# Decoder step on one core: sums of weight blocks added in the SBUF chunk in place of sums kept in DRAM, with five plain column tiles in place of seven

## The chip, the cores and the metric

The kernel runs on one core of one Trainium2 chip. The metric is the device time of one launch in microseconds, the median of three runs. The engines are named as in the profile: PE (TensorE; PEld is its weight load), DVE (VectorE), ACT (ScalarE), POOL (GpSimd) and SP (SyncE, which here only starts transfers).

## What is computed

One decoder layer for 576 tokens (64 sample tokens and 512 prompt tokens) at a model width of 1024. Only the last part, a feed-forward block of width 2816, is touched by the change:

```python
D_FF = int(math.ceil(8 * D_MODEL / 3 / 256) * 256)      # 2816
...
xn = rms_norm(x, g[4])
gate, up = jnp.split(xn @ w_ffn_in, 2, axis=-1)
x = x + rms_norm((jax.nn.silu(gate) * up) @ w_ffn_out, g[5])
```

Ahead of it stand the input projections with a gated convolution and a linear recurrence, a merge, and a cross-attention into 256 memory tokens.

## The kernel before

**Products.** All matrices are float32. A weight chunk of up to 1024 columns by 128 partitions is loaded into a buffer `wraw` (five buffers), split by ACT into a rounded part `whi` and by DVE into the rest `wlo` (four buffers each), and a product takes three matmuls (hi by hi, hi by lo, lo by hi; `mm3`, lines 105 to 108). The activations lie transposed, 128 channels by 576 tokens, in units named `u`, also as a high and a low part.

**Halves.** Tokens are cut in two ways. In the plain way half 0 holds 320 tokens and half 1 holds 256. In the other way both halves, L and R, hold 288.

**The feed-forward block** has 22 column tiles of 128 columns of the gate and the same of the up matrix. The first `NB` = 7 tiles go the plain way (`ffn_half`): for each half, 8 row blocks of gate and of up, so 48 matmuls for half 1 (tokens `F0` to `F6` in `ORDER`, while half 0 is still being normalised) and 48 for half 0 (the loop over `NB` behind it). Each of these 28 steps loads its own chunk of 512 KB.

The other 15 tiles (`ffn_pair`) use seven products of half the depth in place of eight. Row blocks are called E (even) and O (odd), columns G (gate) and U (up). Each product is a block of 4 row blocks by 128 columns times 288 tokens, 12 matmuls. Its weight block is one of EG, OG, OU or a sum: s1 = EU+OU, s2 = EG+EU+OU, s3 = EG+EU, s4 = EG+OG+EU+OU. The order in a tile is EG, s1, s2, OG, s3, s4, OU. Two blocks of 256 KB share a chunk, so two tiles make seven chunks. The tokens' own sums for this are made by `x3_sums` (lines 1342 to 1353) out of x3n, the normalised input.

**Sums of weights.** Before, s1 to s4 are DRAM tensors of 512 by 1920. `sum_task` (line 547) fills them by 32 transfers of 960 KB from POOL's queue, 16 plain copies and 16 with `accum_op=add`, spread over the steps of the first 400 us by `sum_step`. A block of a sum is later loaded by SP like any other weight.

**Order.** Until the first pair step a scheduler places the instructions; steps are written out one after another, and after each step `drain` lets so much background work (norm chains, `x3_sums`) into the program as the step's `budget` allows. From the first pair step on, PE, ACT and DVE follow the written order, while the queues of SP and POOL are still placed by the scheduler. In a pair step (`run_steps`) the engines get, in this order, the 12 matmuls, one small reading of the PSUM bank (`p1` to `p7`), and half of the split of the chunk three ahead (`w_part`); `w_part` also asks for the transfers of later chunks.

**The join of the halves.** The norm of half 0 ends in `rstd_wide` (lines 856 to 860), followed by a multiplication (line 907) and a split (lines 102 and 103) for each of the 8 row blocks of x3n. The first step of half 0 reads them in order.

Of the kernel before, what the change touches and what calls it, by code (L numbers as in the profile page):

```python
# [9 lines left out]
F32 = mybir.dt.float32  # L10
F32R = mybir.dt.float32r
AF = mybir.ActivationFunctionType
ALU = mybir.AluOpType
# [8 lines left out]
DFF = 2816  # L22
# [2 lines left out]

HS = (0, 320)
HW = (320, 256)
NB = 7

# [9 lines left out]


BUD = {"mix": 390, "kv": 306, "q": 480, "o": 2214, "F": 390, "s": 696}

UNIT = 640
NUNITS = 59
# [8 lines left out]
def decoder_step(  # L53
# [7 lines left out]
    nc = tc.nc  # L61
    PE, ACT, DVE, POOL = nc.tensor, nc.scalar, nc.vector, nc.gpsimd
# [38 lines left out]
    def split(hi, lo, src):  # L101
        ACT.copy(hi, src)  # L102
        DVE.tensor_sub(lo, src, f(hi))  # L103
# [74 lines left out]
    def w_dma(upto):  # L178
        while ptr["dma"] <= min(upto, len(wsrc) - 1):
            i = ptr["dma"]  # L180
            srcs, nk, ncol, _ = wsrc[i]
            t = wraw_p.tile([128, 1024], F32, tag="wraw", name="wraw")
            n = nk * ncol // len(srcs)
            for j, src in enumerate(srcs):
                nc.sync.dma_start(out=t[:, j * n:(j + 1) * n].rearrange("p (k c) -> p k c", c=ncol), in_=src)
            raw[i] = t
            ptr["dma"] += 1

# [2 lines left out]
    def w_part(i, b, dma_ahead=2):  # L191

        if i >= len(wsrc) or (b == 0 and ptr["prep"] > i) or (b == 1 and i not in parts):
            return
        assert b or ptr["prep"] == i
        w_dma(i + dma_ahead)
        _, nk, ncol, as_is = wsrc[i]
        if as_is or nk * ncol < 1024:
            if b == 0:
                w_prep(i)  # L200
            return
        if b == 0:
# [51 lines left out]
    def step(w, pe, post=None, budget=4000, prep=True):  # L254
        steps.append((w, pe, post, budget, prep))

    def run_steps():
        nextw = 0
        manual = ExitStack()
        by_hand = False  # L260
        for w, pe, post, budget, prep in steps:
            if w:
                nextw = w[-1] + 1
            if prep in ("pair", "hand"):
                if not by_hand:
                    by_hand = True
                    drain(None)
                    w_prep(nextw - 1 + 2)
                    manual.enter_context(tc.manual_schedule(engines={PE.engine, ACT.engine, DVE.engine}))
                pe(*[ready.pop(i) for i in w])  # L270
                soon, late = post or (None, None)
                if soon:
                    soon()
                if prep == "pair":
                    w_part(nextw - 1 + 3, 0 if w else 1)
                else:
                    w_prep(nextw - 1 + 3)
                if late:
                    late()
                continue  # L280
            if not prep:
                pe()
            else:
                w_prep((w[0] if w else nextw) + 3)
                pe(*[ready.pop(i) for i in w])
            if post:
                post()
            drain(budget)
        manual.close()
# [13 lines left out]
    small = cst.tile([128, 80], F32, name="small")  # L303
# [237 lines left out]
        return g  # L541

    sums = {n: tc.dram_tile([512, DFF - NB * 128], F32, name=f"sum_{n}") for n in ("s1", "s2", "s3", "s4")}

    def sum_task(op, n, src, i):
        def go():
            r = slice(i * 128, i * 128 + 128)
            if src in sums:  # L550
                a = sums[src][r, :]
            else:
                k = 2 * i + (src[0] == "O")
                c = (src[1] == "U") * DFF
                a = w_ffn_in[0][k * 128:(k + 1) * 128, c + NB * 128:c + DFF]
            kw = {"accum_op": ALU.add} if op == "add" else {}
            tc.keep_in_program_order(nc.gpsimd.dma_start(out=sums[n][r, :], in_=a, **kw))
        return go

    sum_tasks = deque(  # L560
        sum_task(op, n, src, i)
        for stage in ((("copy", "s1", "EU"), ("copy", "s3", "EG")), (("add", "s1", "OU"), ("add", "s3", "EU")),
                      (("copy", "s2", "s3"),), (("add", "s2", "OU"),), (("copy", "s4", "s2"),), (("add", "s4", "OG"),))
        for op, n, src in stage for i in range(4))

    def sum_step():
        if sum_tasks:
            step([], sum_tasks.popleft(), budget=0)


    h_h, h_l, vv = [None] * KT, [None] * KT, [None] * KT
    box = {}

# [142 lines left out]
    for c in range(KT):  # L716
        def wi(sec):
            return [w_cols(w_in[0], 0, KT, sec * D + c * 128, 128)]
        if c == 0:
            wi(3), wi(1)  # L720
            step([1], startup, lambda: (in_u(0)[1](), in_hc(0)[1](), softplus()), budget=0, prep=False)
        else:
            step(wi(3), *in_u(c), budget=0)
            step(wi(1), *in_hc(c), budget=3000)
        if c:
            sum_step()
        step(wi(2), *in_hh(c), budget=2000)
        if c:
            sum_step()
        step([], *in_gate(c), budget=2000)  # L730
        step(wi(0), *in_hb(c), budget=9000)
        if c:
            sum_step()


    vs_h, vs_l, z1 = [None] * KT, [None] * KT, [None] * KT
# [12 lines left out]
    def br_rnn(n):  # L749
        def pe(W):  # L750
            box["yr"] = mmt()
            gemm2(box["yr"], W, full(h_h, h_l))

        def post():
            t = box.pop("sgs")
            DVE.tensor_mul(both(t), both(t), box.pop("yr")[:, :, :HN])
            z1[n] = t
            POOL.tensor_copy(small[:, n:n + 1], t[:, 0:1])
            vs_h[n], vs_l[n] = new(F32R), new(F32R)
            split(vs_h[n][:, :T], vs_l[n][:, :T], vv[n][:, :T])  # L760
            free(vv[n])
            if n == 0:
                free(gd, gr_a, gr_x)
            if n == KT - 1:
                free(h_h, h_l)
        return pe, post
# [3 lines left out]
    def br_conv(n):  # L770
        def pe(W):
            box["yc"] = mmt()
            gemm2(box["yc"], W, full(vs_h, vs_l))

        def post():
            t = box.pop("sgs")
            DVE.tensor_mul(both(t), both(t), box.pop("yc")[:, :, :HN])
            DVE.tensor_add(t[:, :T], t[:, :T], z1[n][:, :T])
            POOL.tensor_copy(small[:, n:n + 1], t[:, 0:1])
            z_h[n], z_l[n] = new(F32R), new(F32R)  # L780
            split(z_h[n][:, :T], z_l[n][:, :T], t[:, :T])
            free(t, z1[n])
            if n == KT - 1:
                free(vs_h, vs_l, xn_h, xn_l)
        return pe, post
# [18 lines left out]
    for n in range(KT):  # L804
        step([w_cols(w_in[0], 0, KT, 5 * D + n * 128, 128)], *br_gate(n, "r"))
        step([w_cols(w_rnn_out[0], 0, KT, n * 128, 128)], *br_rnn(n))
        if n == 1:
            step([], state_out)
        sum_step()
    for n in range(KT):  # L810
        step([w_cols(w_in[0], 0, KT, 4 * D + n * 128, 128)], *br_gate(n, "c"))
        step([w_cols(w_conv_out[0], 0, KT, n * 128, 128)], *br_conv(n))
        sum_step()
    assert not sum_tasks


    fb = [[None] * 2 for _ in range(4)]
# [201 lines left out]
    for h in (h0, h1):  # L1019
        for n in range(KT):  # L1020
            step([w_cols(w_mix_out[0], 0, KT, n * 128, 128)], *proj_half(n, fullh(z_h, z_l), h, 1, after_mix),
                 budget=BUD["mix"])
# [337 lines left out]
    def ffn_half(j, up, h):  # L1360
# [15 lines left out]
            free(t)  # L1376
        return pe, post

    def block(name, j):
        if name in sums:  # L1380
            src = sums[name][:, (j - NB) * 128:(j - NB + 1) * 128].rearrange("(k p) c -> p k c", p=128)
        else:
            c = (name[1] == "U") * DFF + j * 128
            src = w_ffn_in[0][:, c:c + 128].rearrange("(k e p) c -> e p k c", p=128, e=2)[name[0] == "O"]
        return src

    FF = {}

# [129 lines left out]
    for a in ORDER.split():  # L1518
        token(a)
    for j in range(NB):  # L1520
        for up in range(2):
# [4 lines left out]
    F = {}  # L1526
# [216 lines left out]
```

## Time and profile before

| | us |
|---|---|
| median of 3 runs | 1157.83 (1157.72 to 1158.13) |
| the profiled execution | 1157.59, of which the span is 1155.8 |
| PE busy | 1134.3 |
| DVE busy | 675.0 |
| ACT busy | 603.2 |
| POOL busy | 146.9 |
| DMA, mean over the span | 165 GB/s |

The span is the profiled part of the execution; the 1.8 us around it are launch and end. Busy times overlap, and a busy PE is not a PE at its peak, because its matmuls are pipelined. TensorE's granted clock is full in all slices of the page.

### The profile page before, as it was taken

What the parts mean: (1) busy time and instruction counts of PE and PEld (TensorE: products, weight loads), DVE (VectorE), ACT (ScalarE), POOL (GpSimd) and SP (SyncE); (2) the same over time, 40 slices, a digit from 0 to 9 for tenths busy, and PEclk for the clock granted to TensorE, in tenths of its full rate; (3) what the DMA queues carried; (4) which work ended last, traced back from release to release, by engine and by line L of the source; (5) the groups of instructions that cost most, each with busy time, mean ns of one, the idle gap of its engine ahead of it and who ended that gap; (6) DMA issues with size and microseconds to landing.
All of it is one profiled execution on the core that took longest, in us unless ns stands there. A gap on an engine that the chain in (4) does not pass through costs nothing.

```text
span 1155.8 us, 21040 instructions
## 1 busy us (share of the span) xinstructions
PE 1134.3 (98%) x8524; PEld 1113.9 (96%) x8524; DVE 675.0 (58%) x1082; ACT 603.2 (52%) x1030; POOL 146.9 (13%) x301
## 2 busy tenths in 40 slices
PE   6999999999999999999999999999999999999996
PEld 4999999999999999999998899999999999999996
DVE  6666666652223335698767777989314663466535
ACT  5665566652122225666557778775325552255543
POOL 4433333212001000022210000000000000000000
PEclk9999999999999999999999999999999999999999
DMA  7556787567547546567675585565444553455702
GB/s 226 171 163 191 178 186 163 177 160 170 173 141 164 147 123 187 147 193 227 196 227 189 192 274 165 155 200 164 129 126 131 164 150 107 118 164 166 227 2 83
DMA packets 256859, 191.13 MB, mean 165 GB/s; under 512 B 9432, under 2 KB 241896, under 8 KB 256634
## 3 DMA queue, kind: packets, MB, share of 16 engines
q1 hardware_dynamic: 249812, 149.95, 43.6%
q0 software_dynamic: 6144, 38.50, 13.0%
q8 instruction: 67, 1.10, 0.4%
q10 hardware_dynamic: 806, 1.34, 0.3%
q14 instruction: 30, 0.25, 0.1%
HBM read 180.36 MB, written 40.85 MB: 191 GB/s over the span
## 4 chain that ended last, share of the span: by engine, by line
PE 94%; DVE 2%; ACT 1%; DMA 1%; issue 1%; POOL 0%; SPq 0%; DVEq 0%; ACTq 0%
PE mm L107 23%; PE mm L108 23%; PE mm L106 23%; PE aux L1397 4%; PE aux L1396 4%; PE aux L1395 4%; PE aux L1225 1%; PE aux L1209 1%; PE aux L106 1%; PE aux L107 1%; PE aux L108 1%; PE mm L1397 1%; PE mm L1396 1%; PE mm L1395 1%; DMA wraw<-in_w_in_dram 1%
## 5 line engine op out<-in xcount | busy, mean ns | idle before, releaser
L106 PE MATMUL mm<-u,whi 128*128 128x288 f32 (+2 forms) x2032 | 605.3, 298 | 0.6 <-ACT u L458 0.6
L107 PE MATMUL mm<-u,whi 128*128 128x288 f32 (+2 forms) x2032 | 601.7, 296 | 0.5 <-DVE u L103 0.5
L108 PE MATMUL mm<-u,wlo 128*128 128x288 f32 (+2 forms) x2032 | 601.7, 296 | 0.2 <-POOL wlo L431 0.2
L103 DVE TENSOR_TENSOR wlo<-wraw,whi 128x1024 fp32r<-128x1024 f32 (+2 forms) x294 | 304.0, 1035 | 215.5 <-ACT whi L102 209.1
L102 ACT CAST whi<-wraw 128x1024 fp32r<-128x1024 f32 (+2 forms) x294 | 261.1, 898 | 286.6 <-PE mm L107 216.6
L107 PEld LDWEIGHTS mm<-u,whi 128*128 128x128 f32 x2032 | 384.5, 189 | 2.4 <-DVE u L103 1.3
L106 PEld LDWEIGHTS mm<-u,whi 128*128 128x128 f32 x2032 | 384.3, 189 | 2.2 <-ACT u L458 1.2
L108 PEld LDWEIGHTS mm<-u,wlo 128*128 128x128 f32 x2032 | 384.0, 189 | 0.8 <-POOL wlo L431 0.6
L1397 PE MATMUL aux<-u,wlo 128*128 128x288 f32 x360 | 106.2, 295 | 0.0
L1396 PE MATMUL aux<-u,whi 128*128 128x288 f32 x360 | 106.1, 295 | 0.0
L1395 PE MATMUL aux<-u,whi 128*128 128x288 f32 x360 | 105.9, 294 | 0.0
L102 ACT CAST u<-u 128x576 fp32r<-128x576 f32 (+6 forms) x117 | 58.9, 532 | 78.6 <-DVE u L640 26.2
L103 DVE TENSOR_TENSOR u<-u,u 128x576 fp32r<-128x576 f32 (+6 forms) x117 | 65.4, 578 | 16.8 <-ACT u L102 16.6
L1397 PEld LDWEIGHTS aux<-u,wlo 128*128 128x128 f32 x360 | 67.6, 188 | 0.0
L1395 PEld LDWEIGHTS aux<-u,whi 128*128 128x128 f32 x360 | 67.6, 188 | 0.0
L1396 PEld LDWEIGHTS aux<-u,whi 128*128 128x128 f32 x360 | 67.6, 188 | 0.0
L103 DVE TENSOR_TENSOR u<-aux,u 128x512 fp32r<-128x512 f32 (+2 forms) x60 | 32.8, 584 | 3.9 <-ACT u L102 3.8
L102 ACT CAST u<-aux 128x512 fp32r<-128x512 f32 (+2 forms) x60 | 28.0, 514 | 6.6 <-DVE u L103 2.1
L106 PE MATMUL aux<-u,u 128*128 128x256 f32 (+1 forms) x96 | 27.8, 294 | 0.0
L108 PE MATMUL aux<-u,u 128*128 128x256 f32 (+1 forms) x96 | 27.7, 289 | 0.0
L107 PE MATMUL aux<-u,u 128*128 128x256 f32 (+1 forms) x96 | 27.6, 289 | 0.0
L1425 ACT ACTIVATE u<-u 128x576 f32<-128x576 f32 x15 | 10.3, 686 | 32.9 <-DVE u L1422 32.9
(284 smaller groups left out, 1193.2 us busy)
## 6 DMA issues: line engine op xcount, KB each, us to landing
wraw<-in_w_in_dram SPq DMA_DIRECT2D x48, 512.0 KB, 4.1
sum_s<-in_w_ffn_in_dram POOLq DMA_DIRECT2D x24, 960.0 KB, 8.3
wraw<-sum_s SPq DMA_DIRECT2D x60, 256.0 KB, 3.3
wraw<-in_w_ffn_in_dram SPq DMA_DIRECT2D x28, 512.0 KB, 4.8
wraw<-in_w_ffn_in_dram SPq DMA_DIRECT2D x45, 256.0 KB, 3.3
wraw<-in_w_mix_out_dram SPq DMA_DIRECT2D x16, 512.0 KB, 3.8
wraw<-in_w_kv_x_dram SPq DMA_DIRECT2D x16, 512.0 KB, 3.8
wraw<-in_w_q_x_dram SPq DMA_DIRECT2D x16, 512.0 KB, 3.9
```

Of the source, the lines that this page charges most:

```text
L102: ACT.copy(hi, src)
L103: DVE.tensor_sub(lo, src, f(hi))
L106: PE.matmul(out, lhsT=wh, rhs=xh, start=start, stop=False)
L107: PE.matmul(out, lhsT=wh, rhs=xl, start=False, stop=False)
L108: PE.matmul(out, lhsT=wl, rhs=xh, start=False, stop=stop)
L1209: PE.transpose(ps[:, d * 256 + i * 128:d * 256 + (i + 1) * 128], kr[i][:, h * 256 + d * 128:h * 256 + (d + 1) * 128], ident)
L1225: PE.matmul(ps[0:m], lhsT=t[:, k * 64:k * 64 + m], rhs=src, **kw)
L1395: PE.matmul(ps, lhsT=wh[:, k, :], rhs=xh[x][:, xs], start=first and i == 0, stop=False, skip_group_check=True)
L1396: PE.matmul(ps, lhsT=wh[:, k, :], rhs=xl[x][:, xs], start=False, stop=False, skip_group_check=True)
L1397: PE.matmul(ps, lhsT=wl[:, k, :], rhs=xh[x][:, xs], start=False, stop=last and i == 3, skip_group_check=True)
L1425: ACT.activation(FF["t"][:, 0:T], FF["t"][:, 0:T], AF.Silu)
```

## The change

`NB` becomes 5, so tiles 5 and 6 go by products too: 17 tiles by products, 5 plain. `ORDER` ends in `F4 D0`, where `D0` drains all the background work that is left, and the budget of an `F` step becomes 800. The DRAM sums, their 32 transfers, the steps that spread them and two one-column POOL copies are gone. A block that is a sum is now built in its half of the `wraw` chunk: SP loads the first part, and POOL's queue adds one, two or three more parts of 256 KB (`accum_op=add`). A pair step asks for transfers 4 chunks ahead of the chunk that it splits, not 2.

```diff
@@ decoder_step
-NB = 7
+NB = 5
...
-    "P3 pA2 oB2 pA1 O5 V6 O4 V7 pA3 XB0 pA0 O6 O7 Z0 oB3 oA0 oA1 oA2 oA3 F0 F1 F2 F3 F4 F5 F6")
+    "P3 pA2 oB2 pA1 O5 V6 O4 V7 pA3 XB0 pA0 O6 O7 Z0 oB3 oA0 oA1 oA2 oA3 F0 F1 F2 F3 F4 D0")
-BUD = {"mix": 390, "kv": 306, "q": 480, "o": 2214, "F": 390, "s": 696}
+BUD = {"mix": 390, "kv": 306, "q": 480, "o": 2214, "F": 800, "s": 696}
@@ w_dma
-                nc.sync.dma_start(out=t[:, j * n:(j + 1) * n].rearrange("p (k c) -> p k c", c=ncol), in_=src)
+                dst = t[:, j * n:(j + 1) * n].rearrange("p (k c) -> p k c", c=ncol)
+                src = src if isinstance(src, list) else [src]
+                nc.sync.dma_start(out=dst, in_=src[0])
+                for more in src[1:]:
+                    nc.gpsimd.dma_start(out=dst, in_=more, accum_op=ALU.add)
@@ run_steps
-                    w_part(nextw - 1 + 3, 0 if w else 1)
+                    w_part(nextw - 1 + 3, 0 if w else 1, 4)
@@ sums, sum_task, sum_tasks, sum_step and their calls: taken out
@@ br_rnn and br_conv
-            POOL.tensor_copy(small[:, n:n + 1], t[:, 0:1])
@@ block
+    PARTS = {"s1": ("EU", "OU"), "s2": ("EG", "EU", "OU"), "s3": ("EG", "EU"), "s4": ("EG", "OG", "EU", "OU")}
+
     def block(name, j):
-        if name in sums:
-            src = sums[name][:, (j - NB) * 128:(j - NB + 1) * 128].rearrange("(k p) c -> p k c", p=128)
-        else:
-            c = (name[1] == "U") * DFF + j * 128
-            src = w_ffn_in[0][:, c:c + 128].rearrange("(k e p) c -> e p k c", p=128, e=2)[name[0] == "O"]
-        return src
+
+        def src(part):
+            c = (part[1] == "U") * DFF + j * 128
+            return w_ffn_in[0][:, c:c + 128].rearrange("(k e p) c -> e p k c", p=128, e=2)[part[0] == "O"]
+        return [src(p) for p in PARTS.get(name, (name,))]
```

**POOL in the pair stage.** Before, POOL's queue ends with the last of four writes of x2a and the four spills of x2; none of these belongs to a weight (`DMASW` is a wait for an earlier transfer of POOL's queue, `DMAHW` for one of SP's).

```order
L1317 DMA x2a_s_100<-u8_8626 128x640 [waits DMASW7_49,DVE_49,Activation_49]
L1473 DMA x2_s_101<-u58_9745 128x512 [waits DMASW0_49,Activation_49]
L1473 DMA x2_s_101<-u5_9804 128x512 [waits DMASW1_49,Activation_49]
L1473 DMA x2_s_101<-u28_9863 128x512 [waits DMASW2_49,Activation_49]
L1473 DMA x2_s_101<-u18_9923 128x512 [waits DMASW3_49,Activation_49]
```

Now the same queue has 119 adding transfers here. These are 12 of the 14 that two tiles take, from the seventh chunk of one pair of tiles on; a line that repeats the chunk of an earlier line and waits for `DMASW` alone is an add onto the result of that earlier add.

```order
L189 DMA wraw_10359<-in_w_ffn_in_dram 128x4x128 [waits DMAHW2_49,DMASW3_49,DVE_49]
L189 DMA wraw_10359<-in_w_ffn_in_dram 128x4x128 [waits DMASW3_49]
L189 DMA wraw_10408<-in_w_ffn_in_dram 128x4x128 [waits DMAHW5_49,DMASW7_49,DVE_49]
L189 DMA wraw_10359<-in_w_ffn_in_dram 128x4x128 [waits DMASW6_49,DMASW4_49]
L189 DMA wraw_10444<-in_w_ffn_in_dram 128x4x128 [waits DMAHW6_49,DMAHW4_49,DVE_49]
L189 DMA wraw_10444<-in_w_ffn_in_dram 128x4x128 [waits DMASW7_49]
L189 DMA wraw_10481<-in_w_ffn_in_dram 128x4x128 [waits DMASW2_49,DMAHW0_49,DMASW1_49,DVE_49]
L189 DMA wraw_10481<-in_w_ffn_in_dram 128x4x128 [waits DMAHW1_49]
L189 DMA wraw_10481<-in_w_ffn_in_dram 128x4x128 [waits DMASW2_49]
L189 DMA wraw_10566<-in_w_ffn_in_dram 128x4x128 [waits DMAHW3_49,DMAHW4_49,DMASW6_49,DVE_49]
L189 DMA wraw_10481<-in_w_ffn_in_dram 128x4x128 [waits DMASW5_49,DMASW3_49]
L189 DMA wraw_10566<-in_w_ffn_in_dram 128x4x128 [waits DMAHW5_49]
```

The queue is in order, so the third line stands behind the wait of the second, though it adds to another chunk.

**DVE at the join of the halves.** Before, the last split of half 0's x3n (the last line, `u1_8592`) had one of the `x3_sums` instructions (line 1345) ahead of it, and two splits of plain chunks.

```order
L103 TENSOR_TENSOR u38_8549<-u54_8547,u48_8548 128x320
L1374 TENSOR_TENSOR u6_9095<-u6_9095,mm_9033 128x256
L907 SCALAR_TENSOR_TENSOR u58_8584<-u8_8626,gT_79,u36_8939 128x320
L103 TENSOR_TENSOR wlo_9112<-wraw_9027,whi_9111 128x1024
L103 TENSOR_TENSOR u22_9099<-u6_9095,u34_9098 128x256
L103 TENSOR_TENSOR u26_8586<-u58_8584,u10_8585 128x320
L907 SCALAR_TENSOR_TENSOR u16_8590<-u8_8626,gT_79,u36_8939 128x320
L1345 TENSOR_TENSOR u15_8481<-u15_8481 128x288
L103 TENSOR_TENSOR wlo_9155<-wraw_9065,whi_9154 128x1024
L103 TENSOR_TENSOR u1_8592<-u16_8590,u24_8591 128x320
```

Now, counted to the same split (`u1_8540`), 14 of the 16 first instructions of `x3_sums` (lines 1311 to 1314 of the changed file) and one of their splits stand ahead of it; these are the last 12 lines.

```order
L1313 SCALAR_TENSOR_TENSOR u5_8435<-u15_8429,u5_8435 128x288
L103 TENSOR_TENSOR u26_8534<-u58_8532,u10_8533 128x320
L1313 SCALAR_TENSOR_TENSOR u40_8483<-u28_8477,u40_8483 128x288
L1311 TENSOR_TENSOR u58_8532<-u58_8532 128x288
L1313 SCALAR_TENSOR_TENSOR u54_8495<-u18_8489,u54_8495 128x288
L873 SCALAR_TENSOR_TENSOR u16_8538<-u8_8574,gT_79,u21_8850 128x320
L1314 SCALAR_TENSOR_TENSOR u40_8483<-u40_8483 128x288
L1312 TENSOR_TENSOR u58_8532<-u16_8538,u58_8532 128x288
L1314 SCALAR_TENSOR_TENSOR u54_8495<-u54_8495 128x288
L1314 SCALAR_TENSOR_TENSOR u5_8435<-u5_8435 128x288
L103 TENSOR_TENSOR u42_9012<-u28_8477,u45_9011 128x576
L103 TENSOR_TENSOR u1_8540<-u16_8538,u24_8539 128x320
```

From the first instruction of `rstd_wide` on DVE (line 859 before) to that last split there are now 37 instructions, both ends counted: 2 of `rstd_wide`, 2 chunk splits of 1024, 8 multiplications, 8 splits of 320, 1 product with its split of 256 (two), 14 of `x3_sums` and 1 split of 576.

## Rows read from the trace of the kernel before

**Rows 1.** The page: busy time of each engine, and the chain that ended last.

```profile
PE 1134.3 (98%) x8524; PEld 1113.9 (96%) x8524; DVE 675.0 (58%) x1082; ACT 603.2 (52%) x1030; POOL 146.9 (13%) x301
PE 94%; DVE 2%; ACT 1%; DMA 1%; issue 1%; POOL 0%; SPq 0%; DVEq 0%; ACTq 0%
```

**Rows 2.** Busy time by stretch: half 1's plain steps, half 0's, the products.

```profile
core 0: us, PE busy (x) PEld busy (x) DVE busy (x) ACT busy (x) POOL busy (x), PEclk, DMA share, GB/s
744.00:763.00 19.00, 19.00 (x159) 18.92 (x159) 18.29 (x26) 13.96 (x21) 2.16 (x4) 1.00 0.73 224
786.00:830.00 44.00, 43.96 (x301) 43.72 (x300) 31.78 (x48) 22.42 (x34) 0.00 (x0) 1.00 0.54 156
870.00:950.00 80.00, 80.00 (x607) 80.00 (x606) 47.30 (x81) 42.52 (x81) 0.00 (x0) 1.00 0.54 155
```

**Rows 3.** Timeline of PE: first step of half 1, of half 0, its wait.

```profile
739.48 0.28 PE L106 MATMUL mm<-u,whi 128*128 128x256 f32 x1
...
781.14 0.31 PE L106 MATMUL mm<-u,whi 128*128 128x320 f32 x1
...
784.87 0.41 PE L107 MATMUL mm<-u,whi 128*128 128x320 f32 x1 [0.34 <-DVE u L103]
```

**Rows 4.** Timeline of ACT at the join: start, us, instruction.

```profile
769.50 0.46 ACT L858 ACTIVATE u<-u 128x320 f32<-128x320 f32 x1
```

**Rows 5.** Timeline of DVE at the join: start, us, instruction.

```profile
773.04 1.47 DVE L907 SCALAR_TENSOR_TENSOR u<-u,gT,u 128x320 f32<-128x320 f32 x3
774.43 1.61 DVE L103 TENSOR_TENSOR u<-u,u 128x320 fp32r<-128x320 f32 x4
775.97 1.47 DVE L907 SCALAR_TENSOR_TENSOR u<-u,gT,u 128x320 f32<-128x320 f32 x3
...
778.17 1.21 DVE L103 TENSOR_TENSOR wlo<-wraw,whi 128x1024 fp32r<-128x1024 f32 x1
779.30 0.47 DVE L103 TENSOR_TENSOR u<-u,u 128x320 fp32r<-128x320 f32 x1
779.70 0.40 DVE L1374 TENSOR_TENSOR u<-u,mm 128x256 f32<-128x256 f32 x1
780.03 0.53 DVE L907 SCALAR_TENSOR_TENSOR u<-u,gT,u 128x320 f32<-128x320 f32 x1
...
785.81 0.44 DVE L1345 TENSOR_TENSOR u<-u 128x288 f32<-128x288 f32 x1
786.17 0.44 DVE L1348 SCALAR_TENSOR_TENSOR u<-u 128x288 f32<-128x288 f32 x1
```

**Rows 6.** Transfers of 256 KB: queue, count, KB, median us to landing.

```profile
wraw<-sum_s SPq DMA_DIRECT2D x60, 256.0 KB, 3.3
...
x_s<-u POOLq DMA_DIRECT2D x8, 256.0 KB, 3.1
...
u<-in_mem_prompt_dram SPq DMA_DIRECT2D x4, 256.0 KB, 2.5
```

**Rows 7.** DMA queues, 880 to 950 us: packets, MB, share of 16 engines.

```profile
q1 hardware_dynamic: 22607, 11.26, 55.4%
```

**Rows 8.** DMA queues and issues, 70 to 100 us, three plain copies to DRAM.

```profile
q0 software_dynamic: 432, 2.95, 29.0%
...
sum_s<-in_w_ffn_in_dram POOLq DMA_DIRECT2D x3, 960.0 KB, 7.1
```

**Rows 9.** DMA queues and issues, 344 to 390 us, four adds in DRAM.

```profile
q0 software_dynamic: 496, 3.44, 38.3%
...
sum_s<-in_w_ffn_in_dram POOLq DMA_DIRECT2D x4, 960.0 KB, 8.4
```

**Rows 10.** Line 557, POOL's transfers for the sums: ns min, median, max.

```profile
L557 POOL DMA_DIRECT2D sum_s<-in_w_ffn_in_dram x24: 517/802/907, 35.0 to 384.8; - x24
```

More of the change, by code (lines that the diff above doesn't have):

```diff
@@ L541, in gate_w @@
         return g
[L545 to L551, printed above, removed]
-            else:
[L553 to L568, printed above, removed]
     h_h, h_l, vv = [None] * KT, [None] * KT, [None] * KT
@@ L724, in decoder_step @@
             step(wi(1), *in_hc(c), budget=3000)
-        if c:
-            sum_step()
         step(wi(2), *in_hh(c), budget=2000)
-        if c:
-            sum_step()
         step([], *in_gate(c), budget=2000)
         step(wi(0), *in_hb(c), budget=9000)
-        if c:
-            sum_step()
     vs_h, vs_l, z1 = [None] * KT, [None] * KT, [None] * KT
@@ L778, in post @@
             DVE.tensor_add(t[:, :T], t[:, :T], z1[n][:, :T])
-            POOL.tensor_copy(small[:, n:n + 1], t[:, 0:1])
             z_h[n], z_l[n] = new(F32R), new(F32R)
@@ L808, in decoder_step @@
             step([], state_out)
-        sum_step()
     for n in range(KT):
@@ L812, in decoder_step @@
         step([w_cols(w_conv_out[0], 0, KT, n * 128, 128)], *br_conv(n))
-        sum_step()
-    assert not sum_tasks
     fb = [[None] * 2 for _ in range(4)]
@@ L1377, in ffn_half @@
         return pe, post
+    PARTS = {"s1": ("EU", "OU"), "s2": ("EG", "EU", "OU"), "s3": ("EG", "EU"), "s4": ("EG", "OG", "EU", "OU")}
     def block(name, j):
-        if name in sums:
-            src = sums[name][:, (j - NB) * 128:(j - NB + 1) * 128].rearrange("(k p) c -> p k c", p=128)
-        else:
-            c = (name[1] == "U") * DFF + j * 128
-            src = w_ffn_in[0][:, c:c + 128].rearrange("(k e p) c -> e p k c", p=128, e=2)[name[0] == "O"]
-        return src
+        def src(part):
+            c = (part[1] == "U") * DFF + j * 128
+            return w_ffn_in[0][:, c:c + 128].rearrange("(k e p) c -> e p k c", p=128, e=2)[part[0] == "O"]
+        return [src(p) for p in PARTS.get(name, (name,))]
     FF = {}
```

## Prediction

> **What bounds the kernel now.** I read the page first. PE is busy for 98% of the span and 94% of the chain that ended last is PE [rows 1], so PE's own instructions set the time. What shortens the time is fewer matmuls; what lengthens it is anything that makes PE wait.
>
> Then the stretches, for what a matmul costs. In each PE is busy all the time at full clock, so length over count is the price [rows 2]: 19.00/159 = 0.1195 us for 256 columns, 44.00/301 = 0.1462 us for 320, 80.00/607 = 0.1318 us for 288.
>
> Then the join of the two token halves, because the change shortens what lies ahead of it. Half 1's plain steps start at 739.48 us, half 0's at 781.14, and the last row block of the first half-0 step begins at 784.87 after a wait of 0.34 us for a DVE split [rows 3]. So the norm of half 0 arrives just in time behind seven tiles of half 1. DVE works almost without a pause there: busy 18.29 of the 19.00 us of [rows 2].
>
> Last the transfers, because the change moves sums into the stage that uses them. Between 880 and 950 us SP's loads of 512-byte rows take 55.4% of the time of the 16 DMA engines [rows 7], while POOL moves nothing there.
>
> **The change, part by part.** *Fewer matmuls.* A plain tile is 48 x (0.1195 + 0.1462) = 12.75 us, a product tile 84 x 0.1318 = 11.07 us. Two tiles change sides: -3.4 us, if PE waits no more than before.
>
> *The join.* Two tiles less of half 1 free PE by 2 x 48 x 0.1195 = 11.5 us: it could start half 0 at 781.14 - 11.5 = 769.6. What it needs is not earlier by as much. ACT's last instruction of the norm ends at 769.96 [rows 4], behind the same work in both kernels, and after it the written program has 37 DVE instructions up to the last split that the first half-0 step needs. Their prices from the starts in [rows 5]: a chunk split 1.13 us (778.17 to 779.30), a multiplication 0.463 (three from 773.04 to 774.43), a split of 320 0.385 (four from 774.43 to 775.97), a product or split of 256 0.33 (779.70 to 780.03), an instruction of `x3_sums` 0.36 (785.81 to 786.17). The split of 576 I take at 0.385 x 576/320 = 0.69, the two of the norm at 0.40 like their width. Sum: 2 x 1.13 + 8 x 0.463 + 8 x 0.385 + 2 x 0.33 + 14 x 0.36 + 0.69 + 2 x 0.40 = 16.2 us. The last split ends at 769.96 + 16.2 = 786.2, 1.3 us after its place before, though PE came 11.5 us sooner. Most of what two tiles freed on DVE (four chunk splits, 4.5 us) goes to the 5.0 us of `x3_sums` that `D0` puts ahead. PE stands for about 13 us between 769.6 and 786.2.
> Against the profiled execution this place is +1.3 us. Behind it four half-0 steps are missing, 96 x 0.1462 = -14.0 us, and two product tiles are added, +22.1 us: +9.4 us in all. If DVE were faster than I count by as much as its four missing chunk splits, the place is at -3 and this term +5; if waits for ACT's casts cost as much again as two chunk splits (2.3 us), +12.
>
> *The removed work.* 32 transfers and 16 POOL copies lie in stages where POOL is at 13% and PE does not wait for it; they cost nothing now and give back nothing. Up to the join PE, ACT and DVE have the same instructions in the same order.
>
> *The sums.* 17 tiles have 119 blocks, so 119 loads and 119 adds of 256 KB. Two tiles are seven chunks, 14 loads and 14 adds, and PE needs 22.1 us for them.
> First the DMA engines. Loads: 0.554 x 70 us = 38.8 us for 11.26 MB [rows 7], 3.44 us per MB, 0.90 us of every engine for a block of 0.262 MB. No add of this shape is in the trace. Adds of long rows are: 0.383 x 46 us = 17.6 us for 3.44 MB, 5.12 us per MB [rows 9]; copies on the same route take 0.290 x 30 us = 8.7 us for 2.95 MB, 2.95 us per MB [rows 8]. The add costs 1.74 times the copy. For 512-byte rows I take the same ratio: 1.57 us. Below, an add costs no more than a load, 0.90. 14 x (0.90 + 1.57) = 34.6 us for what PE does in 22.1.
> Then POOL's queue. Six adds of the 14 wait for the one before them, and five more issues lie between these waits, so the queue needs 6 x landing + 5 x issue. An issue is 0.80 us [rows 10]. A landing lies between 2.5 us, the fastest load of 256 KB, and 8.4 us, an add of 960 KB [rows 6, 9]. It breaks even with PE at (22.1 - 4.0)/6 = 3.0 us, just under the plain 256 KB from POOL, 3.1 us [rows 6]. Taking from the 8.4 us the long add's own movement (0.983 MB x 5.12 = 5.0 us) and putting in 1.57 gives 4.9 us, so 33.4 us. That agrees with the engines' 34.6, and I take 34.6.
> What is queued behind: a late add holds ACT's split of its half chunk, ACT stands in order, so the next readings of the PSUM banks are late, and PE stops two or three blocks later. Five buffers cannot cover a lasting rate. They are full when each of the three groups of product tiles begins, which I count as half a period each: 8.5 - 1.5 = 7 periods x (34.6 - 22.1) = 87.5 us.
> The Trainium skill (DMA: Bandwidth & Descriptors, section "Anatomy of one DMA — SWDGE (gpsimd) path") gives a transfer from POOL as 2.0 us plus its bytes over 436 GB/s; by it a block would land in an estimated 2.6 us, the queue would need 19.6 us, and the sum would be 1167. The trace does not bear it out: 3.1 us for a plain block [rows 6], and 7.1 us for a copy [rows 8] for which the fit has 4.3. The same page ("Issuing engines are not separate DMA queues") says that transfers of all issuing engines run on the same 16 engines, which is how I add loads and adds.
>
> *Sum.* 1157.6 + 9.4 + 87.5 = 1254.5 us. The profiled execution is 0.2 us under the median.
>
> **The rivals.** *Adds nearly hidden.* If adds move as fast as loads, the engines need 14 x 1.80 = 25.3 us, and 7 x 3.2 = 22 us are lost: 1189. If a landing also stays under 3.0 us, nothing is lost and only the join is left: 1167. For it: a block is small, and the longest waits are few. Against it: the 1.74 of [rows 8, 9], and a plain block that already lands at the edge.
> *The waits rule.* If short rows make an add dearer than its bytes, the landing decides. At 7 us, between 4.9 and 8.4, the queue needs 46 us: 7 x 23.9 = 167, so 1334.
> *Faster.* The first condition of the first rival, and with it the join: if the last split of half 0's x3n ended before 776, PE would stand less than 3.4 us and the time would fall below that of before, to 1154 at best. It would need DVE to do in 6 us what I price at 16.2, and its rows hardly vary.
>
> **How the numbers follow.** My forecast, queues that set the pace at 31 to 44 us, 1225 to 1325: 0.58. Adds nearly hidden, 1165 to 1225: 0.27. The waits rule, above 1325: 0.09. Faster: 0.04. Within 0.2%, about the least that a measurement of this kernel can tell from no change (1155.5 to 1160.1): 0.02. Range 1178 to 1325: below it lie 0.06 and some 0.06 of the hidden case, above it 0.09. Faster 0.04, same 0.02, slower 0.94.
>
> **What would show it.** Right: the stretch of the products longer per tile than 11.07 us; ACT casts that wait for transfers from `w_ffn_in`; POOL's transfers starting one after another at the landing of the one before; a PE gap of some 13 us at the join; DMA share near 0.9 or more in the product stage. Wrong, if a 256-KB add lands within 3 us, or if PE starts half 0 at 770 without a gap.

## Result and profile after

The changed kernel takes 1341.12 us (median of 4 runs, 1336.87 to 1343.46) against 1157.98: ratio 1.1577, interval 1.1544 to 1.1609. It was predicted slower, at 1254.5 us; the loss is 183 us, not 97, and the time lies above the range of 1178 to 1325.

From the page of the changed kernel: its engines and its chain, three groups of instructions whose waits matter here, and its 256-KB transfers with the median us from issue to landing:

```profile
PE 1171.3 (87%) x8500; PEld 1144.6 (85%) x8500; DVE 677.9 (51%) x1089; ACT 604.2 (45%) x1036; POOL 274.4 (20%) x372
...
PE 64%; issue 14%; DMA 9%; POOL 7%; DVE 2%; ACT 1%; SPq 0%; POOLq 0%; DVEq 0%; ACTq 0%
...
L102 ACT CAST whi<-wraw 128x1024 fp32r<-128x1024 f32 (+2 forms) x297 | 261.5, 889 | 490.4 <-DMA wraw<-in_w_ffn_in_dram 209.5
...
L1362 PE MATMUL aux<-u,whi 128*128 128x288 f32 x408 | 132.5, 325 | 141.3 <-ACT u L1373 136.3
L189 POOL DMA_DIRECT2D wraw<-in_w_ffn_in_dram x119 | 154.6, 1636 | 317.3 <-DMA wraw<-in_w_ffn_in_dram 290.2
...
wraw<-in_w_ffn_in_dram SPq DMA_DIRECT2D x119, 256.0 KB, 4.7
wraw<-in_w_ffn_in_dram POOLq DMA_DIRECT2D x119, 256.0 KB, 5.9
```

PE is 87% busy, not 98% [rows 1]. Read the waits as one chain: PE's products wait for ACT's reading of a PSUM bank (line 1373, 136.3 us). ACT stands ahead of that reading at a split (line 102) whose chunk has not landed (209.5 us). POOL, which issues the adds (line 189), stands 290.2 us for transfers. What it stands for is in the view of line 189:

```profile
L189 POOL DMA_DIRECT2D wraw<-in_w_ffn_in_dram x119: 1265/1452/2442, 801.2 to 1258.2; - x119
...
who waited for it (us, times):
  POOL wraw L189: 240.1, 51
  ACT whi L102: 209.5, 38
...
DMA to landing us min/median/max: 4.3/5.9/11.1
```

240.1 us of waits are adds that wait for adds, 51 times: the third and fourth parts of sums, three in each of 17 tiles. They are called chained adds below. Issuing an add keeps POOL itself busy for 1.30 us (154.6/119); that is not yet the transfer. The Trainium skill says so too (Perfetto Trace Analysis, section "DMA Instruction — SWDGE (GPSIMD)"): its recorded end is the end of making descriptors, not of moving data; here the data lands 4.3 us or more after the issue.

One period of two tiles (14 adds) in the timeline of POOL, up to the start of the next. Columns: start, us, and in brackets the time that POOL stood before:

```profile
1144.36 3.90 POOL L189 DMA_DIRECT2D wraw<-in_w_ffn_in_dram  x3 [2.55 <-DMA wraw<-in_w_ffn_in_dram]
1151.08 2.59 POOL L189 DMA_DIRECT2D wraw<-in_w_ffn_in_dram  x2 [2.82 <-DMA wraw<-in_w_ffn_in_dram]
1160.17 2.62 POOL L189 DMA_DIRECT2D wraw<-in_w_ffn_in_dram  x2 [6.49 <-DMA wraw<-in_w_ffn_in_dram]
1166.92 2.59 POOL L189 DMA_DIRECT2D wraw<-in_w_ffn_in_dram  x2 [4.12 <-DMA wraw<-in_w_ffn_in_dram]
1173.74 3.91 POOL L189 DMA_DIRECT2D wraw<-in_w_ffn_in_dram  x3 [4.23 <-DMA wraw<-in_w_ffn_in_dram]
1183.99 2.60 POOL L189 DMA_DIRECT2D wraw<-in_w_ffn_in_dram  x2 [6.34 <-DMA wraw<-in_w_ffn_in_dram]
1188.61 3.91 POOL L189 DMA_DIRECT2D wraw<-in_w_ffn_in_dram  x3 [2.03 <-DMA wraw<-in_w_ffn_in_dram]
```

From 1144.36 to 1188.61 are 44.3 us: 18.2 of issues and six stops of 26.0 together. PE needs 22.1 us for the same two tiles when it does not wait. The stretches show where PE lost time:

```profile
core 0: us, PE busy (x) PEld busy (x) DVE busy (x) ACT busy (x) POOL busy (x), PEclk, DMA share, GB/s
763.00:790.00 27.00, 21.18 (x120) 19.77 (x119) 24.24 (x50) 18.98 (x31) 0.00 (x0) 0.82 0.40 118
...
900.00:1062.00 162.00, 104.47 (x690) 101.43 (x689) 53.15 (x91) 46.48 (x86) 55.90 (x43) 0.83 0.88 157
1062.00:1106.00 44.00, 44.00 (x334) 44.00 (x333) 15.31 (x18) 8.75 (x11) 14.63 (x12) 1.00 0.76 143
1106.00:1300.00 194.00, 127.87 (x830) 125.30 (x829) 67.39 (x118) 60.01 (x119) 58.18 (x45) 0.81 0.83 154
```

At the join (763 to 790) PE stands for 5.8 us. In the two stretches that are mostly products (900 to 1062, 1106 to 1300) PE is 64 and 66% busy and the granted clock is 0.83 and 0.81; between them, where `w_ffn_out` is used, PE is full at full clock. At the join PE ends half 1 two tiles sooner, and the timeline of PE there reads:

```profile
770.67 0.28 PE L108 MATMUL mm<-u,wlo 128*128 128x256 f32 x1
774.18 1.09 PE L106 MATMUL mm<-u,whi 128*128 128x320 f32 x2 [3.23 <-ACT u L102]
...
787.00 0.42 PE L107 MATMUL mm<-u,whi 128*128 128x320 f32 x1 [1.50 <-DVE u L103]
```

The last row block of the first half-0 step begins at 787.00, before at 784.87 [rows 3]: 2.1 us later.

### The profile page after: what moved, and what is told of

It is laid out like the page before. It is cut to its first block, busy times and chain, and to the rows that moved or that the text cites. A ratio compares the mean times of both kernels' runs of the same rounds, so it can differ in the third digit from the quotient of the medians.

```text
span 1341.0 us, 21179 instructions
## 1 busy us (share of the span) xinstructions
PE 1171.3 (87%) x8500; PEld 1144.6 (85%) x8500; DVE 677.9 (51%) x1089; ACT 604.2 (45%) x1036; POOL 274.4 (20%) x372
## 4 chain that ended last, share of the span: by engine, by line
PE 64%; issue 14%; DMA 9%; POOL 7%; DVE 2%; ACT 1%; SPq 0%; POOLq 0%; DVEq 0%; ACTq 0%
PE mm L107 18%; PE mm L108 18%; PE mm L106 18%; DMA wraw<-in_w_ffn_in_dram 9%; POOL wraw L189 7%; PE aux L1191 1%; PE aux L1175 1%; PE aux L106 1%; PE aux L107 1%; PE aux L108 1%; PE aux L1362 1%; PE aux L1363 1%; PE aux L1364 1%; DVE wlo L103 0%; DVE u L103 0%
## 5 line engine op out<-in xcount | busy, mean ns | idle before, releaser
L106 PE MATMUL mm<-u,whi 128*128 128x288 f32 (+2 forms) x1968 | 587.9, 299 | 4.3 <-ACT u L102 4.3
L107 PE MATMUL mm<-u,whi 128*128 128x288 f32 (+2 forms) x1968 | 584.2, 297 | 1.7 <-DVE u L103 1.7
L108 PE MATMUL mm<-u,wlo 128*128 128x288 f32 (+2 forms) x1968 | 584.0, 297 | 1.1 <-POOL wlo L435 1.1
L103 DVE TENSOR_TENSOR wlo<-wraw,whi 128x1024 fp32r<-128x1024 f32 (+2 forms) x297 | 303.9, 1024 | 402.9 <-ACT whi L102 399.9
L102 ACT CAST whi<-wraw 128x1024 fp32r<-128x1024 f32 (+2 forms) x297 | 261.5, 889 | 490.4 <-DMA wraw<-in_w_ffn_in_dram 209.5
L106 PEld LDWEIGHTS mm<-u,whi 128*128 128x128 f32 x1968 | 373.7, 190 | 5.9 <-ACT u L102 4.8
L107 PEld LDWEIGHTS mm<-u,whi 128*128 128x128 f32 x1968 | 373.7, 190 | 4.0 <-DVE u L103 2.9
L108 PEld LDWEIGHTS mm<-u,wlo 128*128 128x128 f32 x1968 | 373.2, 190 | 1.7 <-POOL wlo L435 1.5
L1362 PE MATMUL aux<-u,whi 128*128 128x288 f32 x408 | 132.5, 325 | 141.3 <-ACT u L1373 136.3
L189 POOL DMA_DIRECT2D wraw<-in_w_ffn_in_dram x119 | 154.6, 1636 | 317.3 <-DMA wraw<-in_w_ffn_in_dram 290.2
L1362 PEld LDWEIGHTS aux<-u,whi 128*128 128x128 f32 x408 | 84.7, 208 | 147.1 <-ACT u L1373 139.7
L1363 PE MATMUL aux<-u,whi 128*128 128x288 f32 x408 | 128.9, 316 | 0.0
L1364 PE MATMUL aux<-u,wlo 128*128 128x288 f32 x408 | 128.8, 316 | 0.0
L1363 PEld LDWEIGHTS aux<-u,whi 128*128 128x128 f32 x408 | 85.2, 209 | 0.0
L1364 PEld LDWEIGHTS aux<-u,wlo 128*128 128x128 f32 x408 | 85.1, 209 | 0.0
L106 PE MATMUL aux<-u,u 128*128 128x256 f32 (+1 forms) x96 | 27.7, 294 | 0.0
L107 PE MATMUL aux<-u,u 128*128 128x256 f32 (+1 forms) x96 | 27.6, 289 | 0.0
```

The costliest lines, as they stand in the source:

```text
L106: PE.matmul(out, lhsT=wh, rhs=xh, start=start, stop=False)
L107: PE.matmul(out, lhsT=wh, rhs=xl, start=False, stop=False)
L108: PE.matmul(out, lhsT=wl, rhs=xh, start=False, stop=stop)
L189: nc.gpsimd.dma_start(out=dst, in_=more, accum_op=ALU.add)
L1362: PE.matmul(ps, lhsT=wh[:, k, :], rhs=xh[x][:, xs], start=first and i == 0, stop=False, skip_group_check=True)
L1363: PE.matmul(ps, lhsT=wh[:, k, :], rhs=xl[x][:, xs], start=False, stop=False, skip_group_check=True)
```

## Experiments

In all of them "period" is 14 loads and 14 adds (two tiles) in the last group of tiles: half the time between the starts of the 78th and the 106th add, from the timeline of POOL (where one of its rows holds several adds, they are taken in even steps). For the changed kernel it is 45.0 us.

### The two parts of the change, one by one

Without adds (`e1_no_adds`):

```diff
-                for more in src[1:]:
-                    nc.gpsimd.dma_start(out=dst, in_=more, accum_op=ALU.add)
```

> The changed kernel without POOL's 119 adds; a sum block holds only its first part, so its values are not the reference's. Loads, buffers, PE, ACT and DVE stay. Theory (the adds cost what is over 1167): 1157.6 + 9.4 for the join = 1167, PE standing some 13 us between 770 and 787. Rival A (the join costs nothing, PE starts half 0 where half 1 ends): 1154. Rival B (the loads alone are late, because a block is now waited for in other buffers): over 1180.

The join with DRAM sums (`e2_sums_in_dram`), the kernel before with these edits:

```diff
-NB = 7
+NB = 5
-    "... oA3 F0 F1 F2 F3 F4 F5 F6")
+    "... oA3 F0 F1 F2 F3 F4 D0")
-BUD = {... "F": 390, ...}
+BUD = {... "F": 800, ...}
-            tc.keep_in_program_order(nc.gpsimd.dma_start(out=sums[n][r, :], in_=a, **kw))
+            m = (DFF - NB * 128) // 2
+            for s in (slice(0, m), slice(m, 2 * m)):
+                tc.keep_in_program_order(nc.gpsimd.dma_start(out=sums[n][r, s], in_=a[:, s], **kw))
```

> The kernel before with five plain tiles and the changed kernel's order at the join (D0, the budget of F at 800); the sums stay in DRAM, each transfer of a sum row block in two column halves, because a row of 2176 columns is longer than one add takes. It is the other part of the change by itself. Theory: the join alone, +9.4, 1167. Rival: more block products are a gain when the sums cost nothing, 1154.

Measured: 1165.91 (ratio 1.0068, 1.0050 to 1.0086) and 1166.25 us (1.0069, 1.0052 to 1.0086). The join costs 8 us, where 9.4 was summed; the rivals at 1154 and over 1180 are out. The two runs take the same time, one with sums that are made in DRAM in the early stages, the other with no adds at all: the sums in DRAM cost nothing that these runs can tell. Without adds the products run without a pause, shown by this stretch of `e1_no_adds`:

```profile
900.00:1000.00 100.00, 99.85 (x754) 99.61 (x753) 53.91 (x89) 43.29 (x77) 0.00 (x0) 1.00 0.48 140
```

So 1341.1 - 1165.9 = 175 us are the adds.

The sums in SBUF without the join (`e8_sums_only`), the changed kernel with:

```diff
-NB = 5
+NB = 7
-    "... oA3 F0 F1 F2 F3 F4 D0")
+    "... oA3 F0 F1 F2 F3 F4 F5 F6")
-BUD = {... "F": 800, ...}
+BUD = {... "F": 390, ...}
```

> The changed kernel with seven plain tiles and the order and the budget of F of the kernel before: the sums built in SBUF without the change at the join; 105 adds. Theory (the two parts add up, and the sums cost by tiles, 175 us for 17 with half a period free ahead of each group): 175 x 6.5/7 = 162, so 1157.7 + 162 = 1320. Rival (PE's 13 us at the join are lost to late adds anyway, and the join costs nothing when the sums are late): 183 x 6.5/7 = 170, so 1328 or more.

1326.48 us (1.1457, 1.1434 to 1.1480), between the two figures, so it does not tell whether the join costs its 8 us when the sums are late too. It shows that the sums alone cost 168 us with 15 product tiles.

### What in an add costs

Copies of the same blocks in place of adds (`e3_copies`):

```diff
-                    nc.gpsimd.dma_start(out=dst, in_=more, accum_op=ALU.add)
+                    nc.gpsimd.dma_start(out=dst, in_=more)
```

> The changed kernel with the 119 adds turned into plain copies of the same blocks, from the same queue, to the same places, behind the same waits; the values are not the reference's. Theory (it is the add that costs, by what it moves through the 16 DMA engines): a copied block takes the engines what a load takes, 0.97 us, 14 x 1.94 = 27.2 us for two tiles in place of 43, so 1167 + 7 x 5.1 = 1203, the DMA share near 0.8 or below. Rival (the waits of POOL's queue for landings of whatever kind, near 5.9 us): 6 x 5.9 + 5 x 1.45 = 42.7 us, so 1167 + 7 x 20.6 = 1311.

Adds of long rows (`e5_long_rows`):

```diff
-                    nc.gpsimd.dma_start(out=dst, in_=more, accum_op=ALU.add)
+                    nc.gpsimd.dma_start(out=t[:, j * n:(j + 1) * n].rearrange("p (k c) -> p k c", c=256), in_=more,
+                                        accum_op=ALU.add)
...
+            if not first:
+                return w_ffn_in[0][0:256, c - 128:c + 128].rearrange("(k p) c -> p k c", p=128)
...
```

> The changed kernel with each add as 2 rows of 1024 bytes to a partition in place of 4 of 512 (256 columns of two row blocks of the same matrix): the same bytes, adds, order and waits, half the packets; loads as before; the values are not the reference's. Theory (an add costs the engines by its packets, one for each row): 1.06 us, 14 x (0.97 + 1.06) = 28.4 us for two tiles, and the waits decide as with the copies, so 1230 to 1265. Rival (it costs by its bytes): no change, 1330 to 1345.

Half of each add (`e6_half_adds`):

```diff
-                    nc.gpsimd.dma_start(out=dst, in_=more, accum_op=ALU.add)
+                    nc.gpsimd.dma_start(out=dst[:, 0:2, :], in_=more[:, 0:2, :], accum_op=ALU.add)
```

> The changed kernel with each add cut to two of its four row blocks, 128 KB in rows of 512 bytes: half the bytes and half the packets, the same adds, order and waits; the sums are half made, so the values are not the reference's. With the run on long rows it parts bytes from packets. Theory (by packets): the same time as that run, 1230 to 1265. Rival (by bytes): this one falls to there and that one stays.

| run | us | ratio, interval | period | POOL's time for one issue | landing, median |
|---|---|---|---|---|---|
| changed kernel | 1341.12 | 1.1577 (1.1544 to 1.1609) | 45.0 | 1.30 | 5.9 |
| `e3_copies` | 1244.89 | 1.0746 (1.0726 to 1.0765) | 34.2 | 0.75 | 4.3 |
| `e5_long_rows` | 1336.89 | 1.1534 (1.1511 to 1.1558) | 44.4 | 1.21 | 5.9 |
| `e6_half_adds` | 1264.82 | 1.0923 (1.0905 to 1.0942) | 37.5 | 1.21 | 4.7 |

POOL's time for one issue is the busy time of line 189 over 119. The landings, first of the copies, then of the half adds:

```profile
DMA to landing us min/median/max: 3.1/4.3/7.2
```

```profile
DMA to landing us min/median/max: 3.4/4.7/7.6
```

The length of the rows does not matter here: half as many rows, twice as long, left the landing at 5.9 us and the time where it was. In `e5_long_rows` the packets are 964 bytes (6.03 MB in 6257), in the changed kernel 497, in `e3_copies` 3300. Halving the bytes took 1.2 us off the landing and 76 us off the time, so of the two runs' theories the rival held (by bytes). The copies lie between the two figures that I gave: an add costs more than a copy, by issue and by landing, yet copies behind the same waits still cost 79 us. The DMA queues from 960 to 1040 us (q0 is POOL's, q1 SP's; packets, MB, share), first of the changed kernel, then of the copies, then of the long rows:

```profile
q0 software_dynamic: 12658, 6.29, 63.4%
q1 hardware_dynamic: 13593, 6.76, 31.2%
```

```profile
q1 hardware_dynamic: 16189, 8.09, 35.3%
q0 software_dynamic: 1498, 4.94, 20.9%
```

```profile
q0 software_dynamic: 6257, 6.03, 51.8%
```

By these the packets of an add of 0.262 MB take 0.634 x 80 x 0.262/6.29 = 2.11 us on every engine, those of a load 0.97, of a copy 0.89. That is not the pace of adds: packets of one queue overlap in time, as the next part shows.

### The waits or the engines

The adds spread over the queue (`e4_adds_spread`); `todo` holds the adds to come, and of those whose block had none of the last three the one from the earliest chunk goes first; an add of two chunks back is `due` and goes in any case:

```diff
-                for more in src[1:]:
-                    nc.gpsimd.dma_start(out=dst, in_=more, accum_op=ALU.add)
+                if src[1:]:
+                    todo.append([i, dst, src[1:], -9])
...
+            free_now = [p for p in todo if ptr["add"] - p[3] >= 3]
+            if not due and (n >= 2 or not free_now):
+                return
+            p = min(free_now or todo, key=lambda p: p[0] - 0.6 * len(p[2]))
+            tc.keep_in_program_order(nc.gpsimd.dma_start(out=p[1], in_=p[2].pop(0), accum_op=ALU.add))
```

> The changed kernel with the same 119 adds on POOL in another order: the second and third add into a block come at least three adds behind the one before them, so that POOL rarely stands for the landing of the add just issued. Theory 1 (the time of the 16 engines for loads and adds sets the pace): 14 x (0.97 + 2.11) = 43.1 us for two tiles whatever the order, 1167 + 7 x 21.0 = 1314 or more, at a DMA share near 0.95. Theory 2 (POOL's queue sets the pace by its waits): the waits are gone, issues need 14 x 1.45 = 20.3 us, under PE's 22.1, so 1167 to 1190.

1302.19 us (1.1248, 1.1231 to 1.1264), period 41.8. That is nearer to theory 1 (1314 or more) than to theory 2, but what follows takes theory 1 away. In the view of its adds, waits of adds for adds fell to 96.6 us in 29 (240.1 in 51), while waits for DVE's splits came in (line 103, 39.8 us):

```profile
  DMA wraw<-in_w_ffn_in_dram: 178.2, 36
  DVE wlo L103: 39.8, 7
...
who waited for it (us, times):
...
  POOL wraw L188: 96.6, 29
...
DMA to landing us min/median/max: 4.3/6.2/10.3
```

Theory 1 takes 2.11 us for an add. The DMA queues of this run from 1156.5 to 1162.5 us, where adds stand in line and almost no load moves, show another pace:

```profile
q0 software_dynamic: 2092, 1.04, 139.7%
q1 hardware_dynamic: 6, 0.00, 0.2%
```

In 6 us 1.04 MB moved, so an add of 0.262 MB every 1.51 us. The share of POOL's queue alone is 1.40: its packets overlap in time, and 2.11 us of packet time take 1.51 us to go by.

One add for each sum block (`e7_one_add`):

```diff
-                for more in src[1:]:
+                for more in src[1:2]:
```

> The changed kernel with one add for each sum block, 68 in place of 119, so that no add waits for another add; s2 and s4 lack parts, so the values are not the reference's. Theory (the engines' time sets the pace): 14 x 0.97 + 8 x 2.11 = 30.5 us for two tiles, 1167 + 7 x 8.4 = 1226. Rival (the waits of one add for another set it): 8 x 1.45 = 11.6 us of POOL, hidden, 1167 to 1180.

1174.91 us (1.0148, 1.0133 to 1.0163): the rival held. The packet times of loads and adds cannot be added up to a pace. In this stretch of that run (1062 to 1106) the DMA share is over one, 1.14, and PE is nearly full:

```profile
1062.00:1106.00 44.00, 41.86 (x309) 40.79 (x308) 27.68 (x49) 23.14 (x46) 12.94 (x10) 1.00 1.14 232
```

The same 119 adds, one to each block (`e9_flat_adds`):

```diff
-    PARTS = {"s1": ("EU", "OU"), "s2": ("EG", "EU", "OU"), "s3": ("EG", "EU"), "s4": ("EG", "OG", "EU", "OU")}
+    PARTS = {"s1": ("EU", "OU"), "s2": ("EG", "EU"), "s3": ("EG", "EU"), "s4": ("EG", "OG"),
+             "EG": ("EG", "OU"), "OG": ("OG", "EU"), "OU": ("OU", "EU")}
```

> The changed kernel with the same 119 adds dealt out evenly, one to each of the seven blocks of a product tile, so that no add waits for another add; loads, bytes, packets, buffers and the number of adds stay; the sums are of other blocks, so the values are not the reference's. Theory 1 (the engines' time for loads and adds): 14 x (0.97 + 2.11) = 43.1 us for two tiles; where the shares of two queues overlap as far as they did with one add (1.14), 37.8: 1167 + 7 x 15.7 to 21.0 = 1277 to 1314. Theory 2 (POOL's queue, by the adds that wait for the add before them): 14 x 1.3 = 18.2 us of issues, under PE's 22.1, so 1167 to 1190.

1246.52 us (1.0771, 1.0739 to 1.0803), period 34.0: neither theory's figure. No bytes, issue or transfer were taken away, only the waits of adds for adds (and the crowding of adds in some chunks, which this run does not part from them), and 95 of the 175 us are gone; the other 81 are not these waits. Its POOL timeline, the landing of its adds, and the stretch from 1106 to 1160 us:

```profile
1093.55 1.28 POOL L189 DMA_DIRECT2D wraw<-in_w_ffn_in_dram  x1 [1.49 <-DMA wraw<-in_w_ffn_in_dram]
1095.82 1.28 POOL L189 DMA_DIRECT2D wraw<-in_w_ffn_in_dram  x1 [0.99 <-DMA wraw<-in_w_ffn_in_dram]
1098.40 1.28 POOL L189 DMA_DIRECT2D wraw<-in_w_ffn_in_dram  x1 [1.30 <-DMA wraw<-in_w_ffn_in_dram]
...
1119.14 1.28 POOL L189 DMA_DIRECT2D wraw<-in_w_ffn_in_dram  x1 [1.30 <-DMA wraw<-in_w_ffn_in_dram]
```

```profile
DMA to landing us min/median/max: 4.5/11.0/14.9
```

```profile
1106.00:1160.00 54.00, 39.57 (x251) 37.71 (x250) 21.48 (x38) 19.16 (x36) 25.70 (x20) 0.91 1.30 202
```

Eleven adds begin from 1093.55 to 1119.14, one every 2.56 us, in an even beat; the share is 1.30, at 202 GB/s against 166 in the same stretch of the changed kernel. 14 x 2.56 = 35.8 us. (The period is a little shorter, 34.0 us, because its first six adds begin within 6 us.) Adds without loads beside them went at 1.51 us above, so the loads take part in this beat: an estimate from the two is 1.05 us for a load.

Both with four buffers for raw chunks, and with loads three chunks ahead in place of four (`e12_spread_4buf`, `e13_flat_4buf`):

```diff
-    wraw_p = ctx.enter_context(tc.tile_pool(name="wraw", bufs=5))
+    wraw_p = ctx.enter_context(tc.tile_pool(name="wraw", bufs=4))
-                    w_part(nextw - 1 + 3, 0 if w else 1, 4)
+                    w_part(nextw - 1 + 3, 0 if w else 1, 3)
```

> The run with the adds spread, with four buffers for raw chunks in place of five and the loads three chunks ahead in place of four. There 14 loads and 14 adds took 42 us. Theory (a buffer is held from its load over its chain of adds to the cast, and five buffers set that pace): 42 x 5/4 = 52.5 us, 1166 + 7 x 30.4 = 1379. Rival (movement or POOL's queue sets it, not the buffers): 42 us stay, 1295 to 1310.

> The run with one add for each block, with four buffers for raw chunks in place of five and the loads three chunks ahead in place of four; the values are not the reference's. There 14 loads and 14 adds took 34.3 us. Theory (the DMA engines set that pace): the same, 1240 to 1255. Rival (the buffers set it): 34.3 x 5/4 = 42.9 us, 1166 + 7 x 20.8 = 1312.

Flat adds: 1260.99 us (1.0879, 1.0862 to 1.0895), period 36.4. That is 6 us over the theory's 1240 to 1255, but far nearer to its period of 34.3 than to the rival's 42.9. The beat stayed: from 1106.82 to 1158.63 us its POOL timeline has an add every 2.59 us. The landing of an add fell, from a median of 11.0 us to 8.6:

```profile
DMA to landing us min/median/max: 4.6/8.6/11.2
```

```profile
1106.00:1160.00 54.00, 40.03 (x252) 38.19 (x252) 21.88 (x39) 18.82 (x36) 26.98 (x21) 0.91 1.20 204
```

Fewer in flight, each sooner, and the same GB/s: so reads a route that is full at this mix of loads and adds. That it is the 16 engines, and not another part of the way that loads and adds share, is not shown. Spread adds: 1348.99 us (1.1647, 1.1624 to 1.1670), period 44.8, between the two figures. Buffers, or the loads that come later with them, have a part in its pace, but don't set it alone.

### The join

Both from the kernel before, with DRAM sums: `e10_join_no_d0` is `e2_sums_in_dram` with

```diff
-    "... F0 F1 F2 F3 F4 D0")
+    "... F0 F1 F2 F3 F4")
-BUD = {... "F": 800, ...}
+BUD = {... "F": 1600, ...}
```

> The run with the sums in DRAM and five plain tiles, without the last D0 and with the budget of F at 1600: the 14 instructions of x3_sums that were counted ahead of half 0's first splits come later, in the half-0 steps. Theory (5.0 us of the join are theirs): the first half-0 step is complete 5.0 us sooner, 1166.2 - 5.0 = 1161. Rival (DVE has no room later, the products then wait for t_h): 1166 or more.

and `e11_six_tiles` is the kernel before with

```diff
-NB = 7
+NB = 6
-    "... oA3 F0 F1 F2 F3 F4 F5 F6")
+    "... oA3 F0 F1 F2 F3 F4 F5")
```

> The kernel before with six plain tiles, sums in DRAM, all else as it was. Theory (the join keeps half 0 near its old place): two chunk splits fewer bring the last split of the first half-0 step 2.3 us forward, 48 half-0 matmuls are missing, 7.0 us, one product tile is added, 11.1: +1.8, 1159.5. Rival (the join is free): 12.75 less 11.07 gained, 1156.1.

1159.67 us (1.0010, 1.0000 to 1.0019) and 1158.80 us (1.0008, 0.9999 to 1.0018). Both are within 1.5 us of their theories; against the kernel before, timed beside them at 1158.25, they are 1.4 and 0.6 us over, where 3.5 and 1.8 were expected. Without `D0`, and with the larger budget, the wait that ended at 787.00 in the changed kernel ends at 774.95, and the next long one comes behind it:

```profile
774.95 0.41 PE L107 MATMUL mm<-u,whi 128*128 128x320 f32 x1 [0.70 <-DVE u L103]
...
788.35 0.39 PE L106 MATMUL mm<-u,whi 128*128 128x320 f32 x1 [1.41 <-ACT u L1375]
```

The join is then nearly closed, yet the time is not the 1154 of a free one; beyond the 1.41 us at 788 the rest was not traced. Five, six or seven plain tiles come to the same; no version beat the kernel before.

## Why the prediction was right and wrong

**Direction and mechanism: right.** Products wait for chunks whose adds are late, by the chain of queues that was given.

**The join: right in size.** Summed +9.4, measured +8.1 (`e1_no_adds`) and +8.5 (`e2_sums_in_dram`). The picture was wrong in part: not one gap of 13 us, but one of 3.2 us and then half 0's matmuls as row blocks came in, 5.8 us of standing in all; the last row block of the first step began 2.1 us late, where 1.3 was summed.

**The engines' term: right in size, and in part by luck.** 14 loads and adds were put at 34.6 us; in the beat of flat adds they take 35.8, and with flat adds the loss is 81 us, where 87.5 was summed. The add was put at 1.57 us, and adds alone went at 1.51. But that price was a share of packet time carried over from long DRAM transfers, and in the changed kernel the packet time of an add reads 2.11 us; no row showed that such a figure would be a pace. Had I summed the rows of that trace, 14 x (0.97 + 2.11) = 43 us, I would have got close to the changed kernel's 45 for a wrong reason: `e7_one_add` needs 30.5 us by these prices and lost 9 us in all, and flat adds undercut 43 with the same transfers.

**POOL's queue: the step that failed.** "33.4 us. That agrees with the engines' 34.6, and I take 34.6." The formula, 6 x landing + 5 x issue, was the right one; two values in it were too small, and so the agreement on which 34.6 was taken was chance. The issue is 1.30 us, not 0.80: that row [rows 10] mixes copies and adds of few long rows, and here an add's issue is 0.55 us above a copy's of the same block. The landing is 5.9 us, not 4.9: taking the long add's movement off its 8.4 us left 3.4 us, and the runs agree (half an add lands 1.2 us sooner, so an estimate of 5.9 less 2.4 is 3.5), but the movement put back was 1.57 in place of 2.4. So 6 x 5.9 + 5 x 1.30 = 41.9 us, 6.0 of the 8.5 us more by the landing and 2.5 by the issue. The formula gives 34.3 for half adds and 29.6 for copies; the periods are 45.0, 37.5 and 34.2, each some 3 to 5 us above it, and what these are was not traced. 7 x (45.0 - 22.1) = 160, near the 175 that was measured, where 87.5 was summed. The seven periods of the prediction hold for most: 1166 + 7 x (period - 22.1) is within 15 us of every run with 119 transfers from POOL but the one of spread adds with four buffers (24).

**The rival on the waits** (46 us, 1334) came nearest to the 45.0 us and 1341, and I gave it 0.09. That the landing decides held. Its condition did not, that short rows make an add dear: `e5_long_rows` has other rows and the same time. Its 46 us also came from a landing of 7 us and an issue of 0.80, not from the 5.9 and 1.30 that were measured. **Adds nearly hidden** needed a landing under 3.0 us; no add of 256 KB whose landing was read came under 4.3. By the Trainium skill (DMA: Bandwidth & Descriptors, section "Anatomy of one DMA — SWDGE (gpsimd) path") a block lands in an estimated 2.6 us; the runs show 4.3 for a copy from DRAM to SBUF and 5.9 for an add, and the measurement decides.

**Not as additive as summed.** Taking away the waits of adds for adds gives 95 us, by flat adds. Spreading them gave only 39 us; what holds that run at 41.8 us stays open: 29 adds still waited for adds, and buffers have a part in it (`e12_spread_4buf`). What the lowered granted clock of the product stretches cost was not tried. A matmul took 104.47/690 = 0.151 us there, against 0.132; PE stood for a third of these stretches and may have had that time, but no run shows it.

## What to carry to other kernels

A queue that issues transfers in order and waits between them is to be summed like an engine with its own time: add issue and landing over a period, from rows of the same kind of transfer, and do not drop that sum because another one agrees. Chained adds into one buffer cost a whole landing each (5.9 us here). Sums that were made in DRAM in an early stage, when nothing waited, cost nothing (1166.25 us with them, 1165.91 without any adds), and here they stay the better choice. If sums must be made late, avoid chains: 68 adds, one to a block, cost 9 us; 119, one to a block, 81; 119 with 51 of them chained, 175.

## What was not expected of the hardware

- An add and a copy of the same block from the same queue differ in kind: issue 1.30 and 0.75 us, landing 5.9 and 4.3 us, mean packets of 497 bytes and 3.3 KB.
- The share of the DMA engines can be more than one: 1.30 for two queues with flat adds, 1.40 for POOL's queue alone with spread adds. So a share near 0.9, as in the changed kernel, is not yet a full route, and prices from shares cannot be added up to a pace: an add had 2.11 us of packet time and went every 1.51 us without loads beside it.
- After the gap of 3.2 us at the join the granted clock was 0.50, the lower level of 1.2 GHz, all through this stretch of 3.9 us:

```profile
774.10:778.00 3.90, 3.82 (x13) 3.55 (x14) 3.90 (x11) 1.87 (x6) 0.00 (x0) 0.50 0.34 100
```
